# A backbone of two layers on one core: the way from the first attention into its FFN put in a set order, the latents' norm first, two inner tiles multiplied feature by feature, unread modulation rows left out

## The chip, the cores and the metric

The kernel runs on one core of one Trainium2 chip. The metric is the device time of one execution in microseconds, as the median of several runs.

A core has five engines that run beside each other: TensorE (PE in the profile) multiplies and writes into PSUM, VectorE (DVE) and ScalarE (ACT) work element by element, GpSimd (POOL) here adds and issues some transfers, SyncE (SP) issues loads. An engine runs its instructions in the order in which they stand in its queue; one that waits holds up all that stand behind it.

## The reference, cut to what matters

512 latent tokens `x` and 256 context tokens `ctx`, of 1024 features, go through two layers. Each layer has attention and a SwiGLU feed-forward network (FFN, 2816 inner features), each behind a norm that is scaled and shifted by modulation vectors. Latents and context have modulation of their own.

```python
for layer in range(2):
    mod_x = split(silu(c)     @ ada_w[layer] + ada_b[layer], 6)     # for latents
    mod_c = split(silu(c_ctx) @ ada_w[layer] + ada_b[layer], 6)     # for the context
    h_x = modulate(rmsnorm(x, norm_g[layer, 0]), mod_x[0], mod_x[1])
    h_c = modulate(rmsnorm(ctx, norm_g[layer, 0]), mod_c[0], mod_c[1])
    o_x, o_c = mixer(h_x, h_c, ...)                                 # o_c only in layer 0
    x = x + mod_x[2] * o_x
    h_x = modulate(rmsnorm(x, norm_g[layer, 1]), mod_x[3], mod_x[4])
    x = x + mod_x[5] * ((silu(h_x @ w1) * (h_x @ w3)) @ w2)
    if layer == 0:
        ctx = ctx + mod_c[2] * o_c
        h_c = modulate(rmsnorm(ctx, norm_g[layer, 1]), mod_c[3], mod_c[4])
        ctx = ctx + mod_c[5] * ((silu(h_c @ w1) * (h_c @ w3)) @ w2)
return rmsnorm(x, final_g)
```

In layer 1 the context gets no output, so of its six modulation rows only the first two (`mod_c[0]`, `mod_c[1]`) are read.

## The kernel before

**Layout.** Activations lie with features on the 128 partitions, in KT = 8 tiles `k` of 128 features, and tokens along the free dimension: NX = 512 latents and NC = 256 context tokens. `xr` and `cr` are the residual streams, `hx` and `hc` (tiles `hb0` to `hb7`) the normed inputs. Everything is held as a high and a low part, and each product is made of three, `mm3`: high weight by high input (L209), high by low (L210), low by high (L211).

**Weights.** A `Stream` S loads raw weight tiles of 128 x 1024 in a fixed order (SP), and makes the two parts: high by ACT (L160 or L198), low by DVE as raw minus high (L161 or L199, the tile `wl`). A second way, `split_by_dma`, takes DVE out of it: ACT writes minus the rounded raw values into the low tile (L203), a transfer issued on POOL adds raw to them in place (L204, `wl<-raw`), and ACT writes the high part (L205).

**The end of the first attention.** The output projection has eight chunks `m` of 128 output features (`wo_chunk`). The second half of each is multiplied here: for `t` = 0 to 3 the latents' products of m = 2t and 2t + 1 (the context's of the chunks m > 1 are held back). Each ends with a residual addition on DVE (L1324), after which ACT squares the residual and DVE or POOL add the squares up (`sq_sum`: L334, L338, L340). Two sums are kept apart, so the statistics product (`rstd_of`, L308) has two matmuls for the latents and two for the context. Then `rstd_from` and for each feature tile `h_make`: a product with scale and rstd on DVE (L352), the high part on ACT (L353), the low part on DVE (L354).

**Into the FFN.** Inner tiles `j` of 128 features: `plain_tile` multiplies w1 and w3 of the tile with latents and context, takes silu (L1518 or L1520) and multiplies (L1522), and splits the result g. For j = 0 PE gets sixteen keep-busy matmuls (L219) that are issued behind the last context product. j = 0 to 3 are done in this way, then comes `seven` for each later pair of inner tiles: seven products of 384 tokens instead of eight (L1533 to L1535), from sums of token halves (`token_sums`, L1468 to L1486, with the splits of T) that DVE and ACT make while tiles 2 and 3 are multiplied.

**Modulation rows.** The modulation vectors of the later steps are made on the side: for a load of 128 x 1024 of the transposed `ada_w` DVE multiplies with the latents' conditioning row and sums (L271), then with the context's (L272). I call each of the two a half row. Three groups of them lie near the change: four late rows of layer 0 under the output projection (`late_rows`), four at the start of the FFN (`rows(4, ...)`), the other rows of layer 1 spread over the FFN up to 911 us.

**What sets the order.** The program is written in Python under a scheduler that places the instructions of each engine by its own estimates, within the dependencies; `issue_after` adds one. PSUM has eight banks. Each new tile in a bank waits for the last reader of the tile before it. SBUF memory is handed on in the same way.

## Time and profile before

| | us |
|---|---|
| median of 3 runs (1574.49 to 1578.61) | 1577.53 |
| the profiled execution | 1577.44 |
| its span | 1575.6 |
| PE, DVE, ACT, POOL busy | 1540.2, 1228.7, 728.8, 257.1 |
| PE idle between 415.2 and 490.1 (end of the output projection, norms, inner tiles 0 and 1) | 4.15 |
| PE idle between 490.1 and 523.4 (inner tiles 2 and 3) | 0.0 |

All times in a profile are from one execution, counted from the start of the span. An instruction's time has a tail in which the next one has begun: wide matmuls (512 columns) follow each other every 0.23 us and show 0.39. Line numbers are those of the kernel before where nothing else is said. The changed file is longer, and a line that is the same in both has another number there: L1324 there is L1344, or L1417 where it is written out anew; L1468 is L1673, L1522 is L1723, L271 and L272 are both L274, and L1533 is L1734.

### The profile page before, as it was taken

The numbers are of one execution on the slowest core, as the hardware profiler recorded it, in microseconds if no ns is written. First come the engines' busy times: TensorE is split into PE (matmuls) and PEld (weight loads), VectorE is DVE, ScalarE is ACT, GpSimd is POOL, SyncE is SP. The second block draws the span as 40 slices with busy tenths as digits, with TensorE's granted clock in tenths as the row PEclk, the third lists the DMA queues.
The fourth block names the chain that finished last, engine by engine and source line by source line (L and its number), as shares of the span: only waits on it lengthen the run. The fifth ranks groups of instructions, "written<-read, shape, count | busy, mean of one in ns | idle before, by whom it ended". The sixth has DMA issues, their size and how long they took to land.

```text
span 1575.6 us, 25696 instructions
## 1 busy us (share of the span) xinstructions
PE 1540.2 (98%) x10021; PEld 1369.0 (87%) x10021; DVE 1228.7 (78%) x2097; ACT 728.8 (46%) x1241; POOL 257.1 (16%) x329
## 2 busy tenths in 40 slices
PE   9999999999999999999999999999999999999997
PEld 5898988877778999999999998877778899989897
DVE  4768788967698789869799777677666887869686
ACT  4556554445354523433425244366655543425344
POOL 1033213552010000010100002255430000000000
PEclk9999999999999999999999999999999999999999
DMA  9422254633235465485766752311113442422321
GB/s 357 113 61 85 83 162 138 203 111 101 65 120 165 117 178 157 139 209 160 203 178 162 214 149 92 91 55 41 42 41 87 128 147 81 134 68 94 121 81 54
DMA packets 68625, 196.41 MB, mean 125 GB/s; under 512 B 6692, under 2 KB 19140, under 8 KB 68504
## 3 DMA queue, kind: packets, MB, share of 16 engines
q1 hardware_dynamic: 58040, 159.95, 31.9%
q0 software_dynamic: 9488, 33.51, 9.8%
q8 instruction: 79, 1.29, 0.3%
q10 hardware_dynamic: 976, 1.31, 0.3%
q14 instruction: 42, 0.34, 0.1%
HBM read 161.04 MB, written 4.86 MB: 105 GB/s over the span
## 4 chain that ended last, share of the span: by engine, by line
PE 51%; DVE 6%; issue 5%; DMA 4%; ACT 1%; POOL 0%; SPq 0%; DVEq 0%; POOLq 0%; ACTq 0%
PE f L1535 4%; PE f L1534 4%; PE f L1533 4%; PE f L2208 4%; PE f L2209 4%; PE f L2210 4%; PE f L1574 2%; PE f L1575 2%; PE f L1576 2%; PE lin L1870 2%; PE s L1759 2%; PE f L2262 2%; PE f L2263 2%; PE f L2261 2%; PE t L410 2%
## 5 line engine op out<-in xcount | busy, mean ns | idle before, releaser
L198 ACT ACTIVATE wh<-raw 128x1024 fp32r<-128x1024 f32 (+1 forms) x96 | 92.1, 977 | 235.1 <-DVE raw L539 88.7
L199 DVE TENSOR_TENSOR wl<-raw,wh 128x1024 fp32r<-128x1024 f32 (+1 forms) x96 | 106.9, 1120 | 39.7 <-ACT wh L198 39.1
L209 PE MATMUL lin<-hb,wh 128*128 128x512 f32 (+1 forms) x352 | 121.7, 347 | 5.5 <-DVE k L379 2.0
L210 PE MATMUL lin<-hb,wh 128*128 128x512 f32 (+1 forms) x352 | 120.2, 342 | 0.4 <-DVE hb L1303 0.4
L211 PE MATMUL lin<-hb,wl 128*128 128x512 f32 (+1 forms) x352 | 119.0, 338 | 0.0
L271 DVE SCALAR_TENSOR_TENSOR junk<-raw,tables 128x1024 bf16<-128x1024 f32 x80 | 99.4, 1243 | 19.1 <-DMA raw<-in_ada_wT_dram 18.7
L204 POOL DMA_DIRECT2D wl<-raw x39 | 34.1, 873 | 443.9 <-ACT wl L203 404.1
L1574 PE MATMUL f<-g,wh 128*128 128x512 f32 (+1 forms) x304 | 102.4, 338 | 0.4 <-DVE s L1563 0.4
L1575 PE MATMUL f<-g,wh 128*128 128x512 f32 (+1 forms) x304 | 102.8, 339 | 0.0
L2209 PE MATMUL f<-hb,wh 128*128 128x256 f32 x360 | 101.6, 283 | 0.0
L2208 PE MATMUL f<-hb,wh 128*128 128x256 f32 x360 | 101.4, 283 | 0.0
L2210 PE MATMUL f<-hb,wl 128*128 128x256 f32 x360 | 101.2, 283 | 0.0
L1576 PE MATMUL f<-g,wl 128*128 128x256 f32 (+1 forms) x304 | 101.1, 337 | 0.0
L1535 PE MATMUL f<-hb,wl 128*128 128x384 f32 x288 | 96.3, 334 | 0.0
L1533 PE MATMUL f<-hb,wh 128*128 128x384 f32 x288 | 96.2, 334 | 0.0
L1534 PE MATMUL f<-hb,wh 128*128 128x384 f32 x288 | 96.2, 334 | 0.0
L209 PEld LDWEIGHTS lin<-hb,wh 128*128 128x128 f32 x352 | 66.6, 189 | 16.9 <-issue 2.7
L1535 PE MATMUL f<-T,wl 128*128 128x384 f32 x216 | 72.3, 336 | 2.2 <-DVE wl L199 2.2
L210 PEld LDWEIGHTS lin<-hb,wh 128*128 128x128 f32 x352 | 66.7, 189 | 8.2 <-DVE hb L1303 0.6
L211 PEld LDWEIGHTS lin<-hb,wl 128*128 128x128 f32 x352 | 66.6, 189 | 7.5
L1534 PE MATMUL f<-T,wh 128*128 128x384 f32 x216 | 72.2, 334 | 0.0
L1533 PE MATMUL f<-T,wh 128*128 128x384 f32 x216 | 72.2, 334 | 0.0
(540 smaller groups left out, 4843.3 us busy)
## 6 DMA issues: line engine op xcount, KB each, us to landing
raw<-in_w_dram SPq DMA_DIRECT2D x132, 512.0 KB, 3.7
raw<-in_ada_wT_dram SPq DMA_DIRECT2D x80, 512.0 KB, 3.8
wl<-raw POOLq DMA_DIRECT2D x41, 512.0 KB, 6.5
raw<-in_w_ab_dram SPq DMA_DIRECT2D x24, 512.0 KB, 4.3
raw<-in_w_c_dram SPq DMA_DIRECT2D x12, 512.0 KB, 4.3
raw<-in_ada_w_dram SPq DMA_DIRECT2D x8, 512.0 KB, 9.2
nb<-in_na_bias_dram POOLq DMA_DIRECT2D x16, 256.0 KB, 3.2
raw<-in_wo_ab_dram SPq DMA_DIRECT2D x8, 512.0 KB, 3.9
```

The costliest lines, as they stand in the source:

```text
L209: nc.tensor.matmul(ps, wh(k), xh(k), start=k == 0, stop=False)
L210: nc.tensor.matmul(ps, wh(k), xl(k), start=False, stop=False)
L211: end = nc.tensor.matmul(ps, wl(k), xh(k), start=False, stop=k == n - 1)
L1533: nc.tensor.matmul(ps, wh(k), b[:, 0, :], start=k == 0, stop=False)
L1534: nc.tensor.matmul(ps, wh(k), b[:, 1, :], start=False, stop=False)
L1535: nc.tensor.matmul(ps, wl(k), b[:, 0, :], start=False, stop=k == 3)
L1574: nc.tensor.matmul(ps, hi, g[:, 0, cols[v]], start=first, stop=False)
L1575: nc.tensor.matmul(ps, hi, g[:, 1, cols[v]], start=False, stop=False)
L1576: nc.tensor.matmul(ps, lo, g[:, 0, cols[v]], start=False, stop=last)
L2208: nc.tensor.matmul(ps, wh(k), b[:, 0, :], start=k == 0, stop=False)
L2209: nc.tensor.matmul(ps, wh(k), b[:, 1, :], start=False, stop=False)
L2210: nc.tensor.matmul(ps, wl(k), b[:, 0, :], start=False, stop=k == 3)
```

## The change

1. The order between the last chunks of the output projection and the end of tiles 0 and 1 is written out by hand for PE, DVE and ACT (`manual_schedule`).
2. The latents' residuals come first; their squares are summed on ACT and DVE alone, into one sum, so that one matmul makes the statistics (L1485). The context's chunks 2 to 7 are multiplied while the norm's chain runs.
3. w1 and w3 of inner tiles 0 and 1 are placed in memory of the attention's work tiles (`spare`, tile `w0`), and split with an ACT copy and an accumulating transfer on POOL (L1456, L1457, L1459). Their products with the latents are made for one feature tile at a time, as each h is there (`first_products`, L1541), into four banks `s`. The context's products follow (`lin`). The sixteen keep-busy matmuls go.
4. The attention's PSUM pools stay open until tiles 0 and 1 are done; the FFN's eight banks are opened behind that, on the same memory.
5. In layer 1 the half rows of the context for s = 2 to 5 are left out (`sides`). Three late rows instead of four are under the output projection, one more is left to the FFN (`rows(5, ...)`, now behind `token_sums` in the program).
6. The next conversions of weights (pair p = 1 and one of p = 2) are issued behind the norm's end (`behind_norm`), and the two rope loads of the next norm behind a residual addition.

PE behind the last context product of the output projection, before (`lin`: a bank of the attention, `f`: a bank of the FFN, `hb0`, `hb1`: normed inputs, `wh` and `wl`: high and low weights, f_4836 and f_4838 w1 and w3 of tile 0, f_4977 w1 of tile 1):

```order
L211 MATMUL lin_4689<-hb7_121,wl_4488 128x256
L219 MATMUL f_4836<-ones_96,ident_95 128x128 x16
L308 MATMUL t_4703<-ns_a_4704,ones_96 128x256
L308 MATMUL t_4703<-ns_a_4705,ones_96 128x256
L209 MATMUL f_4836<-hb0_114,wh_4860 128x512
L209 MATMUL f_4838<-hb0_114,wh_4864 128x512
L209 MATMUL f_4977<-hb0_114,wh_4981 128x512
L210 MATMUL f_4836<-hb0_114,wh_4860 128x512
```

Now the first product L1541 stands right behind the context's last one (`s_4697<-hb0_114,w0_4546`); twelve products for features 0 and 1 of tile 0 come, and then tile 1 begins. Their end (s_4697 is tile 0, s_4698 tile 1; w0_4546 holds both parts of w1 of tile 0, 4547 and 4548 the parts of w3; 4549 and 4550 those of w1 of tile 1, 4551 and 4552 those of w3):

```order
L1541 MATMUL s_4697<-hb1_115,w0_4548 128x512
L1541 MATMUL s_4697<-hb1_115,w0_4546 128x512
L1541 MATMUL s_4697<-hb1_115,w0_4547 128x512
L1541 MATMUL s_4698<-hb0_114,w0_4549 128x512
L1541 MATMUL s_4698<-hb0_114,w0_4551 128x512
L1541 MATMUL s_4698<-hb0_114,w0_4550 128x512
L1541 MATMUL s_4698<-hb0_114,w0_4552 128x512
```

The keep-busy products and the context's statistics no longer stand ahead of the first h. The 16th of the new products is the first that reads w0_4552, the low part of w3 of tile 1.

ACT at the norm's end, now (`ns_h`: input times scale and rstd; rows L1456 write a low part, L1459 a high one; no such rows stood there before):

```order
L1456 ACTIVATE w_4550<-raw 128x1024
L1459 CAST w_4549<-raw 128x1024
L1400 ACTIVATE ns_h<-res 128x256
L1525 ACTIVATE hb_114<-ns_h,mod_110 128x512
L1525 ACTIVATE hb_115<-ns_h,mod_110 128x512
L1456 ACTIVATE w_4552<-raw 128x1024
L1525 ACTIVATE hb_116<-ns_h,mod_110 128x512
L1459 CAST w_4551<-raw 128x1024
```

The last low part stands behind the latents' features 0 and 1, and what POOL adds to it comes behind that.

DVE between the context's last h and the token sums, before (half rows: L271, L272 with the output `junk`; `q<-f`: the product of silu and w3's output; `g`: its low part; L1468: the first token sum):

```order
L271 SCALAR_TENSOR_TENSOR junk_4817,mod0_110<-raw_4820,tables_72 128x1024
L272 SCALAR_TENSOR_TENSOR junk_4817,mod0_110<-raw_4820,csr1_4791 128x1024
L271 SCALAR_TENSOR_TENSOR junk_4817,mod0_110<-raw_4824,tables_72 128x1024
L272 SCALAR_TENSOR_TENSOR junk_4817,mod0_110<-raw_4824,csr1_4791 128x1024
L1522 TENSOR_TENSOR q_5101<-f_4979,q_5101 128x512
L274 TENSOR_TENSOR mod0_110<-mod0_110,adab_104 128x16
L1522 TENSOR_TENSOR q_5101<-f_4980,q_5101 128x256
L199 TENSOR_TENSOR wl_5181<-raw_4996,wh_5180 128x1024
L199 TENSOR_TENSOR g_4835<-q_5101,g_4835 128x768
L1468 TENSOR_TENSOR q_5111<-hb0_114 128x768
```

Now, from tile 1's product on:

```order
L274 SCALAR_TENSOR_TENSOR junk_4985,mod0_110<-raw_4981,tables_72 128x1024
L1723 TENSOR_TENSOR q_4994<-s_4698,q_4994 128x512
L536 TENSOR_TENSOR res_4975<-raw_5141 128x512
L1723 TENSOR_TENSOR q_4994<-lin_4915,q_4994 128x256
L274 SCALAR_TENSOR_TENSOR junk_4985,mod0_110<-raw_4981,csr1_4983 128x1024
L537 TENSOR_TENSOR raw_5141<-raw_5141,raw_5139 128x512
L199 TENSOR_TENSOR wl_5401<-res_4975,wh_5400 128x512
L199 TENSOR_TENSOR g_4986<-q_4994,g_4986 128x768
L274 SCALAR_TENSOR_TENSOR junk_4985,mod0_110<-raw_5097,tables_72 128x1024
```

All eight half rows stood ahead of tile 1's product; now three of ten do, and seven come behind it, the last five of them between the token sums.

The core of the diff:

```diff
+    def sides(l, s):
+        return 1 if l and s > 1 else 2
...
     def ada_rows(l, s, k, cs, raw, junk):
-        col = mod[l][:, s, :, k : k + 1]
-        nc.vector.scalar_tensor_tensor(junk, raw, 1.0, cs[0], op0=ALU.mult, op1=ALU.mult, accum_out=col[:, 0])
-        nc.vector.scalar_tensor_tensor(junk, raw, 1.0, cs[1], op0=ALU.mult, op1=ALU.mult, accum_out=col[:, 1])
+        col, n = mod[l][:, s, :, k : k + 1], sides(l, s)
+        for i in range(n):
+            nc.vector.scalar_tensor_tensor(junk, raw, 1.0, cs[i], op0=ALU.mult, op1=ALU.mult, accum_out=col[:, i])
...
+    def behind_norm(fn):
+        def f(raw):
+            with tc.issue_after(norm_end[0].ins):
+                return fn(raw)
+        return f
...
-                        late_rows += row_pieces(1)
+                        late_rows.append(row_pieces((2, 1, 0, 0)[m - 4]))
...
-        r = rstd_of(tp(), sq_sum(xr, nmap), D, nmap)
-        for k in range(KT):
-            h_make(k, hx[k], xr[k], r, 0, 1, 0, nmap)
-        weights0()
-        for m, w in held:
-            wo_chunk(m, w, "c", 4)
...
+        def conversion(hi, lo):
...
+            def low():
+                nc.scalar.activation(lo, raw, AF.Copy, scale=-1.0)
+                nc.gpsimd.dma_start(f32(lo), raw, accum_op=ALU.add)
+            return low, lambda: nc.scalar.copy(hi, raw)
+
+        w10, w30, w11, w31 = (conversion(*z) for z in spare)
+        by_hand = ExitStack()
+        by_hand.enter_context(tc.manual_schedule(engines={ENG.PE, ENG.DVE, ENG.Activation}))
...
+        nc.tensor.matmul(psx, ones, ax[0], start=True, stop=True)
...
+        first_ps = [[[s[:, NX * i : NX * i + NX], None] for i in range(2)] for s in (sp2(), sp2())]
+
+        def first_products(*jk):
+            for j, k in jk:
+                for kind in ("hh", "lh", "hl"):
+                    for i in range(2):
+                        w = wslice(first_w[2 * j + i][kind == "lh"])
+                        nc.tensor.matmul(
+                            first_ps[j][i][0], w(k), hx[k][:, int(kind == "hl"), :],
+                            start=k == 0 and kind == "hh", stop=k == KT - 1 and kind == "hl",
+                        )
+
+        h_t(0, 0)
+        h_t(1, 0)
+        w31[0]()
+        h_lo(0, 0)
+        to_residual(5, 1, pc[5])
+        h_t(2, 0)
+        w31[1]()
+        square(5, 1)
+        h_lo(1, 0)
+        first_products((0, 0))
...
+        first_products((0, 1), (1, 0))
...
+        first_products((0, 6), (1, 5), (0, 7), (1, 6), (1, 7))
...
         def plain_tile(j, g):
...
-            if j == 0:
-                keep_busy(ps[0][0], 16, before[0])
...
+            if j < 2:
+                ps = first_ps[j]
             else:
...
-        rows(4, h_made[-1][1])
+        g = g_tile()
+        for j in range(2):
+            plain_tile(j, g)
+        banks.close()
+        for i in range(8):
+            fpp.pools.append(st.enter_context(tc.tile_pool(name=f"f_ps{i}", bufs=1, space=PSUM, reuse_waits="tile")))
+        token_sums()
+        rows(5, h_made[-1][1])
```

More of the change, by code (lines that the diff above doesn't have):

```diff
@@ L221, in keep_busy @@
                 nc.tensor.matmul(ps[:, 0:P], ident, ones, start=True, stop=True)
-    before = [None]
     def wo_slices(t, i):
@@ new lines, in tile_trunk @@
+        first_products((0, 2), (1, 1))
+        add_square(6, 1)
+        add_halves(1)
+        h_t(5, 0)
+        h_lo(4, 0)
+        first_products((0, 3), (1, 2))
+        add_square(7, 1)
+        psc = tp()[:, 0:NC]
+        first_products((0, 4), (1, 3))
+        nc.tensor.matmul(psc, ones, ac[0], start=True, stop=True)
+        h_t(6, 0)
+        h_lo(5, 0)
+        first_products((0, 5), (1, 4))
+        chain = stats(psc, NC, place[2][:, 0:NC], rstds[1], place[2][:, NC:NX])
+        next(chain)
@@ L1399, in tile_trunk @@
+        by_hand.close()
     with ExitStack() as st:
```

234 lines of the change are left out of this document (182 added, 52 removed).

## The prediction

> **What bounds the kernel now.** The page first: which engine is busy, and which one the chain that ended last runs over.
>
> ```profile
> span 1575.6 us, 25696 instructions
> PE 1540.2 (98%) x10021; PEld 1369.0 (87%) x10021; DVE 1228.7 (78%) x2097; ACT 728.8 (46%) x1241; POOL 257.1 (16%) x329
> PE 51%; DVE 6%; issue 5%; DMA 4%; ACT 1%; POOL 0%; SPq 0%; DVEq 0%; POOLq 0%; ACTq 0%
> ```
>
> TensorE (PE) is busy 98% of the span, so a change pays only through its idle time and through products that are not work. Next the table by stage around the change; after the stage's bounds stand its length, then busy time and instructions of PE, PEld, DVE, ACT and POOL, the granted clock, DMA share and GB/s.
>
> ```profile
> 415.20:490.10 74.90, 70.75 (x405) 60.86 (x404) 62.42 (x103) 32.61 (x54) 7.83 (x7) 1.00 0.40 118
> 490.10:523.40 33.30, 33.30 (x194) 29.47 (x193) 31.28 (x56) 14.87 (x23) 1.72 (x2) 1.00 0.45 132
> 475.00:500.00 25.00, 25.00 (x154) 22.49 (x153) 18.00 (x30) 10.52 (x14) 1.80 (x2) 1.00 0.73 212
> 500.00:525.00 25.00, 25.00 (x148) 22.38 (x147) 24.58 (x45) 12.69 (x21) 1.72 (x2) 1.00 0.35 85
> 725.00:750.00 25.00, 23.28 (x134) 22.94 (x133) 23.34 (x41) 10.33 (x12) 0.87 (x1) 1.00 0.48 135
> ```
>
> The passage, from the second half of the output projection to the end of tiles 0 and 1, runs from 415.2 to 490.1; PE idles 74.90 - 70.75 = 4.15 us in it. Tiles 2 and 3 (490.1 to 523.4) have no gap, but DVE is busy 31.28 of 33.30 us under them. So two engines are close to the bound here, one behind the other. The timeline of PE shows the places (start, duration, then in brackets the idle time before):
>
> ```profile
> 442.99 1.88 PE L308 MATMUL t<-ns_a,ones 128*128 128x512 f32 x4
> 449.01 3.73 PE L219 MATMUL f<-ones,ident 128*128 128x128 f32 x32
> 453.48 1.10 PE L308 MATMUL t<-ns_a,ones 128*128 128x256 f32 x4 [0.73 <-DVE ns_a L340]
> 457.36 0.50 PE L210 MATMUL f<-hb,wh 128*128 128x512 f32 x1 [1.60 <-DVE hb L354]
> 490.12 0.40 PE L209 MATMUL f<-hb,wh 128*128 128x512 f32 x1
> 523.49 0.34 PE L1533 MATMUL f<-hb,wh 128*128 128x384 f32 x1
> ```
>
> The sixteen keep-busy products take 3.73 us, and the largest gap is 1.60. Tile 2 starts at 490.12, the first "seven" product (that of token pair 2 and 3) at 523.49. These two times are the marks of my sum.
>
> **What can be gained in the passage.** Gaps 4.15, keep-busy products 3.73, and half of the two statistics products ((1.88 + 1.10) / 2 = 1.49): 9.4 us, if PE then never waits. All other products stay.
>
> **New waits, one by one.** (1) In the new order the latents' statistics product comes behind the context products of m = 2 and 3 (about 440.2 on this axis), then the context products of m = 4 to 7, then the first product L1541, which needs the first h. The rows on its way:
>
> ```profile
> 444.91 0.69 ACT L315 ACTIVATE ns_t<-t,epst 128x512 f32<-128x512 f32 x1 [0.92 <-PE t L308]
> 446.36 0.61 ACT L317 ACTIVATE ns_y<-ns_t 128x512 f32<-128x512 f32 x1
> 447.81 0.62 ACT L318 ACTIVATE ns_t<-ns_y 128x512 f32<-128x512 f32 x1
> 456.57 0.74 DVE L354 SCALAR_TENSOR_TENSOR hb<-ns_h,mod,hb 128x512 fp32r<-128x512 f32 x1
> 454.03 0.72 ACT L353 ACTIVATE hb<-ns_h,mod 128x512 fp32r<-128x512 f32 x1 [2.25 <-DVE ns_h L352]
> 478.11 1.06 ACT L203 ACTIVATE wl<-raw 128x1024 fp32r<-128x1024 f32 x1
> ```
>
> The product takes 0.94 with its tail, ACT 0.69 + 0.61 + 0.62, DVE three rows of 0.74, ACT 0.72 for h: 5.8, and 1.4 for DVE rows of the context that stand in between and for hand-overs: h is there at 447.4. PE has 0.66 of statistics and 4 x 1.44 of context products (a tile's pass of 24 wide and 24 narrow products is 33.3 / 4 = 8.3, so a narrow one is 0.12, a wide one 0.23): 446.6. A wait of 0.8. Waits for residual rows and the next h rows stay near those of before: 1.4 together.
>
> (2) The weights of tiles 0 and 1 get their low halves not from DVE (four subtractions of 1.2 us, freed) but from an ACT copy and an accumulating DMA issued on POOL. The last of the four (w3 of tile 1) has its copy (1.06) behind h of features 0 and 1 on ACT, so from 448.0 to 449.0, and is issued at about 449.3. The 16th L1541 product needs it, 15 x 0.23 and two short waits behind the first: 451.3. What does such a DMA take? Count, KB, median us to landing, for the whole page, then for the stages 460 to 500 and 500 to 540:
>
> ```profile
> wl<-raw POOLq DMA_DIRECT2D x41, 512.0 KB, 6.5
> wl<-raw POOLq DMA_DIRECT2D x2, 512.0 KB, 7.0
> wl<-raw POOLq DMA_DIRECT2D x5, 512.0 KB, 4.5
> ```
>
> At 449 one weight load and the copy of the conditioning row run beside it in the new order, less than from 460 on, more than from 500 on: I take 5.5, with bounds 4.5 and 7.0. The product waits 449.3 + 5.5 - 451.3 = 3.5 us (2.5 to 5.0). [...] Sum for tiles 0 and 1: -9.4 + 0.8 + 1.4 + 3.5 = -3.7, so they end at 486.4 instead of 490.1.
>
> (3) Tile 2's first product takes a bank of the freed attention pools, the one that tile 1's gate product (L1723) reads last. Before, eight separate banks were there and nothing waited. The elementwise work costs:
>
> ```profile
> 489.99 0.68 DVE L1522 TENSOR_TENSOR q<-f,q 128x512 f32<-128x512 f32 x1
> 480.00 0.96 DVE L199 TENSOR_TENSOR g<-q,g 128x768 fp32r<-128x768 f32 x1 [0.50 <-ACT g L198]
> 479.07 0.83 ACT L198 ACTIVATE g<-q 128x768 fp32r<-128x768 f32 x1
> 481.06 0.60 ACT L1520 ACTIVATE q<-f 128x512 f32<-128x512 f32 x1 [1.16 <-DVE g L199]
> 474.13 1.22 DVE L272 SCALAR_TENSOR_TENSOR junk<-raw,csr 128x1024 bf16<-128x1024 f32 x1
> ```
>
> After tile 1's last product: tile 0's high half 0.83 on ACT, its low half 0.96 on DVE, then tile 1's silu 0.60, a half row of the modulation that stands in between (started about 0.7 before the silu is through, so another 0.6), the multiplication 0.68, with 0.3 of hand-overs: 4.0 us. Tile 2 starts at 490.4, against 490.12. The gain of the passage is used up at that place; bounds 2.7 (no half row in the way) and 5.3 (two).
>
> (4) Tiles 2 and 3 take their 33.3 us and are done at 523.7. What they cover before is DVE's token sums (L1468 and on) and the splits of T:
>
> ```profile
> 487.57 1.22 DVE L271 SCALAR_TENSOR_TENSOR junk<-raw,tables 128x1024 bf16<-128x1024 f32 x1 [4.19 <-DMA raw<-in_ada_wT_dram]
> 493.43 1.83 DVE L1468 TENSOR_TENSOR q<-hb 128x768 f32<-128x768 f32 x2
> 497.50 0.69 DVE L534 TENSOR_TENSOR res<-raw 128x512 f32<-128x512 f32 x1 [1.78 <-DMA raw<-in_w_dram]
> 519.88 0.85 ACT L1520 ACTIVATE q<-f 128x512 f32<-128x512 f32 x2
> ```
>
> Before, all eight half rows of this place had run by 490, in a stretch where DVE had time to wait 4.19 us for a load. Tile 2's silu, which frees the bank of the first seven product, came at 519.88, behind the T splits; with 0.65 for its first half it was through at 520.5, only 3.0 us ahead of PE's need at 523.49. In the changed order the rows come through two fresh buffers whose loads wait for memory that tile 1 reads until about 478, and seven half rows stand behind tile 1's multiplication, among the token sums: 7 x (1.22 + 0.04 read-out and gap) = 8.8 us. From tile 1's multiplication (490.4): the rest of the tile and one half-size conversion 3.0, the half rows 8.8, sums and splits as before (519.88 + 0.65 - 493.43 - 1.78 of waiting = 25.3, less 2.0 of conversions now ahead of it, plus 1.2 for one now in it), and 1.3 for L540, which waits for an accumulating DMA that has become late with the rest: 528.0. PE waits 4.3 us there, and starts at 528.0 instead of 523.49: +4.5. Bounds: L540's wait 0 to 3 and the landing in (2), together -2.3 to +3.2, and (3)'s, up to +1.3: +4.5.
>
> (5) Later. In layer 1 the context's half of rows s = 2 to 5 is left out: 32 of the half rows of this group (min, median, max in ns, first and last start).
>
> ```profile
> L272 DVE SCALAR_TENSOR_TENSOR junk<-raw,csr x52: 1207/1218/1229, 474.1 to 910.9; 128x1024 bf16<-128x1024 f32 x52
> 575.00:600.00 25.00, 24.53 (x142) 24.21 (x141) 23.45 (x40) 9.47 (x10) 1.74 (x2) 1.00 0.70 200
> 600.00:625.00 25.00, 24.57 (x141) 22.33 (x140) 23.21 (x41) 8.50 (x9) 0.87 (x1) 1.00 0.51 141
> 734.29 0.44 PE L1535 MATMUL f<-T,wl 128*128 128x384 f32 x1 [1.72 <-DVE wl L199]
> ```
>
> That takes 39 us from DVE up to 911. PE could use it in three places: 0.47, 0.43 and 1.72 us of idle time. So 0 to -2.6; I take half, -1.3, since DVE also starts this stretch 4 us later. The rope tables' loads and the five conversions put behind the norm lie under 33 us of products: nothing.
>
> **Sum.** +4.5 - 1.3 = +3.2. The profiled execution took 1577.4 (span 1575.6 and 1.8 around it), 0.1 below the median of 1577.53, so I forecast 1580.5. Within its own bounds (-2.3 and -1.3 below, +4.5 and +1.3 above): 1577 to 1586. A change of 0.3% (4.7 us, 1572.8 to 1582.3) is about what can be told from none.
>
> **Rivals.** *The gain stays (faster).* The half rows load earlier or fall into DVE's wait before tile 0's silu (about 475 to 481, when it has no other work), and the token sums are then covered. The half row drops out of (3), the 8.8 out of (4), so PE no longer waits at the first seven product: 486.4 - 1.0 (a landing of 4.5) + 2.7 + 33.3 = 521.4, that is -2.1; the later -2.6 makes it 1572.7, and if DVE's 4.9 us freed in (2) close the small waits of (1) too, 1571.3. For it: the 4.19 us that DVE waits for a load now. Against it: their order on DVE, which is fixed.
>
> *The accumulating DMA or the row loads come late (slower).* The stage 460 to 500 has a median of 7.0 where the row loads run at the same time, and 475 to 500 has the highest DMA share, 0.73. With 7.0 at all of them the product in (2) waits 1.5 more and L540 1.5 more, and a late row load holds DVE's queue for 1 to 2: +3.2 + 4.5, 1585. It decides from a landing of about 6.3 on.
>
> *The clock falls (slower).* The keep-busy products go, and two waits of 4 us come. The clock as the profile grants it (third column from the right), at the start, at the gaps of the passage and at the end:
>
> ```profile
> 12.00:16.00 4.00, 3.37 (x6) 1.74 (x7) 2.11 (x5) 2.19 (x4) 0.00 (x0) 0.62 1.04 384
> 453.00:457.00 4.00, 2.06 (x7) 1.16 (x7) 4.00 (x7) 2.97 (x6) 0.00 (x0) 1.00 0.87 294
> 1568.00:1572.00 4.00, 0.00 (x0) 0.00 (x0) 3.35 (x6) 0.23 (x1) 0.00 (x0) 0.68 0.29 97
> ```
>
> With 1.94 us idle of four the clock stays at 1.00, with four idle it falls (0.68), and at 12 to 16 it is 0.62 though PE is busy. If each of the two waits is followed by such a stretch, four microseconds at 0.62, each costs 1.5 more: 1580.5 + 3.0 = 1583.5. [...]
>
> **Chances.** Within 0.3% (the sum as it stands): 0.42. The gain stays: 0.22, faster. Late DMAs 0.24 and the clock 0.12: slower, 0.36. The range of 1571 to 1588 leaves out about 0.1 at each end: it reaches below the first rival and holds the second with the clock's price on top.
>
> **What would show it.** In the profile after: no L219; the first L1541 product near 447 and a PE wait of about 3.5 us for a DMA of w<-raw fifteen products later; tile 2's first product near 490 behind a DVE L1723; half rows (L274) among L1673 and L1681 from 491 to 509; a PE wait of about 4 us at the first L1734 product, near 528. Step (2) is wrong if that DMA lands in under 4 us or over 7, step (4) if PE has no wait of over 2 us at L1734, step (5) if the time between that product and 911 shrinks by over 2.6 us or grows. The clock rival needs a granted clock under 1.00 right after one of these waits.

## The result, and the profile after

| | us |
|---|---|
| predicted | 1580.5 (1571 to 1588) |
| after, median of 6 runs (1584.92 to 1603.48) | 1593.36 |
| before, median of 6 runs beside them (1574.49 to 1579.97) | 1577.38 |
| after / before | 1.0106, interval 1.0072 to 1.0139 |
| the profiled execution of after, and its span | 1594.26, 1592.5 |

The change makes the kernel 16 us slower. The forecast had it within 0.3% and missed by 12.9 us, outside its range.

The top of the page of after, in answer to the first fence of the prediction:

```profile
span 1592.5 us, 25552 instructions
PE 1543.6 (97%) x9985; PEld 1371.8 (86%) x9985; DVE 1190.2 (75%) x2035; ACT 733.4 (46%) x1245; POOL 255.9 (16%) x329
PE 64%; DMA 13%; DVE 10%; issue 8%; ACT 4%; SPq 0%; POOL 0%; DVEq 0%; ACTq 0%; POOLq 0%
```

PE has 36 matmuls less and yet 3.4 us more busy time, and 13.5 us more of idle time (1592.5 - 1543.6 = 48.9 against 35.4). DVE lost 38.5 us of work, near the 39 foreseen, and the end came no earlier. In the last chain, DMA went from 4% to 13%.

The timeline of PE in after, the rows that answer to the marks (start, duration, the idle time before it in brackets; L1541 are the products made feature by feature, L209 at 493.35 is tile 2's first, L1734 the first "seven" product):

```profile
448.55 4.03 PE L1541 MATMUL s<-hb,w 128*128 128x512 f32 x14 [0.60 <-ACT hb L1525]
452.94 0.50 PE L1541 MATMUL s<-hb,w 128*128 128x512 f32 x1 [0.36 <-DMA w<-raw]
456.52 11.65 PE L1541 MATMUL s<-hb,w 128*128 128x512 f32 x39 [3.08 <-DMA w<-raw]
493.35 0.79 PE L209 MATMUL f<-hb,wh 128*128 128x512 f32 x1 [3.67 <-DVE q L1723]
533.48 0.60 PE L1734 MATMUL f<-hb,wh 128*128 128x384 f32 x1 [3.66 <-ACT q L1721]
927.22 0.69 PE L1736 MATMUL f<-hb,wl 128*128 128x384 f32 x1 [4.82 <-DMA wl<-raw]
```

Three of the four waits are those of the forecast, at their places and in their sizes (3.4, 3.67, 3.66; forecast 3.5, 4.0, 4.3). The fourth, at 927, was not in it. But the marks are late: tile 2 starts 3.2 us later than before (493.35 against 490.12), the first seven 10.0 (533.48 against 523.49), the span ends 16.9 later. So 10.0 us are lost ahead of the first seven and 6.9 behind it. The clock tells more. The columns are those of the prediction's stage table, in windows of 2 us behind the waits:

```profile
456.00:458.00 2.00, 1.48 (x4) 1.19 (x5) 2.00 (x4) 0.72 (x1) 0.00 (x0) 0.50 0.81 291
460.00:462.00 2.00, 2.00 (x6) 1.52 (x6) 0.00 (x0) 0.00 (x0) 0.00 (x0) 0.52 0.20 76
462.00:464.00 2.00, 2.00 (x11) 1.62 (x10) 0.00 (x0) 0.00 (x0) 0.00 (x0) 1.00 0.00 0
494.00:496.00 2.00, 2.00 (x6) 1.59 (x5) 0.00 (x0) 0.00 (x0) 0.00 (x0) 0.50 0.72 272
534.00:536.00 2.00, 2.00 (x8) 2.00 (x7) 2.00 (x4) 1.30 (x2) 0.00 (x0) 0.50 0.00 0
928.00:930.00 2.00, 2.00 (x8) 2.00 (x8) 2.00 (x5) 1.27 (x2) 0.00 (x0) 0.50 0.00 0
```

Behind each of the four waits the granted clock is 0.50 (third column from the right), up to 461.9 behind the first: six products in 2 us instead of eleven. PE counts as busy there. PE's busy time at 0.50, multiplied by the half that the clock lacks, is 2.70, 3.06, 1.71 and 2.87 us, 10.34 in all.

Now the wait at 927. POOL's timeline in after (L204 is the accumulating transfer, L1652 the rope loads):

```profile
892.78 0.87 POOL L204 DMA_DIRECT2D wl<-raw  x1 [7.57 <-ACT wl L203]
919.04 1.13 POOL L1652 DMA_DIRECT2D tables<-in_rope_dram  x2 [25.39 <-DVE junk L274]
920.14 0.96 POOL L204 DMA_DIRECT2D wl<-raw  x1
```

The ACT copy ahead of that last transfer, and the DVE instruction that waits for it, from the timelines of ACT and DVE:

```profile
912.34 1.05 ACT L203 ACTIVATE wl<-raw 128x1024 fp32r<-128x1024 f32 x1
927.20 0.69 DVE L540 TENSOR_TENSOR raw<-res,raw 128x512 f32<-128x512 f32 x1 [5.73 <-DMA wl<-raw]
```

And POOL at the same place before, where the rope loads are L1446 and L1447:

```profile
903.46 0.87 POOL L204 DMA_DIRECT2D wl<-raw  x1 [20.04 <-ACT wl L203]
910.19 0.57 POOL L1446 DMA_DIRECT2D tables<-in_rope_dram  x1 [5.86 <-DVE junk L271]
918.03 0.90 POOL L204 DMA_DIRECT2D wl<-raw  x1 [6.72 <-ACT wl L203]
```

The transfer that goes out at 903.46 before, ahead of the rope loads, stands behind them after. The loads overwrite the conditioning row that the last half row reads, so they wait 25.39 us for it, and the L204 behind them is issued at 920.14 although its ACT copy was through at 913.4. Counted over the program, 37 L204 are ahead of the rope loads before, 36 after. In these rows POOL issues in the order of its queue, the loads at 919.04 and the L204 behind them at 920.14: loads that nobody needed yet held up a transfer for which PE waited 4.82 us and DVE 5.73.

### The profile page after: what moved, and what is told of

It is laid out like the page before. It is cut to its first block, busy times and chain, and to the rows that moved or that the text cites. A ratio compares the mean times of both kernels' runs of the same rounds, so it can differ in the third digit from the quotient of the medians.

```text
span 1592.5 us, 25552 instructions
## 1 busy us (share of the span) xinstructions
PE 1543.6 (97%) x9985; PEld 1371.8 (86%) x9985; DVE 1190.2 (75%) x2035; ACT 733.4 (46%) x1245; POOL 255.9 (16%) x329
## 4 chain that ended last, share of the span: by engine, by line
PE 64%; DMA 13%; DVE 10%; issue 8%; ACT 4%; SPq 0%; POOL 0%; DVEq 0%; ACTq 0%; POOLq 0%
DMA wl<-raw 6%; PE f L2415 4%; PE f L2414 4%; PE f L2413 4%; PE lin L209 3%; PE f L1736 3%; PE lin L211 3%; PE f L1735 3%; PE f L1734 3%; PE lin L210 3%; PE t L412 3%; PE f L1775 3%; PE f L1777 3%; PE f L1776 3%; DVE junk L274 2%
## 5 line engine op out<-in xcount | busy, mean ns | idle before, releaser
L199 DVE TENSOR_TENSOR wl<-raw,wh 128x1024 fp32r<-128x1024 f32 (+1 forms) x96 | 106.9, 1122 | 46.4 <-ACT wh L198 45.8
L209 PE MATMUL lin<-hb,wh 128*128 128x512 f32 (+1 forms) x344 | 118.8, 346 | 4.8 <-DVE k L381 2.5
L210 PE MATMUL lin<-hb,wh 128*128 128x512 f32 (+1 forms) x344 | 118.1, 343 | 0.5 <-DVE hb L1323 0.5
L274 DVE SCALAR_TENSOR_TENSOR junk<-raw,tables 128x1024 bf16<-128x1024 f32 x77 | 95.7, 1243 | 14.1 <-DMA raw<-in_ada_wT_dram 13.9
L204 POOL DMA_DIRECT2D wl<-raw x39 | 34.0, 873 | 439.0 <-ACT wl L203 421.6
L1734 PE MATMUL f<-hb,wh 128*128 128x384 f32 x288 | 98.0, 340 | 3.7 <-ACT q L1721 3.7
L1735 PE MATMUL f<-hb,wh 128*128 128x384 f32 x288 | 98.0, 340 | 0.0
L209 PEld LDWEIGHTS lin<-hb,wh 128*128 128x128 f32 x344 | 65.1, 189 | 15.4 <-DVE k L381 3.3
L1734 PE MATMUL f<-T,wh 128*128 128x384 f32 x216 | 72.1, 334 | 0.0
L210 PEld LDWEIGHTS lin<-hb,wh 128*128 128x128 f32 x344 | 65.1, 189 | 8.1 <-DVE hb L1323 0.7
```

The lines of the kernel that those rows point to most:

```text
L209: nc.tensor.matmul(ps, wh(k), xh(k), start=k == 0, stop=False)
L210: nc.tensor.matmul(ps, wh(k), xl(k), start=False, stop=False)
L1734: nc.tensor.matmul(ps, wh(k), b[:, 0, :], start=k == 0, stop=False)
L1735: nc.tensor.matmul(ps, wh(k), b[:, 1, :], start=False, stop=False)
```

## The experiments

All runs in one table; the interval belongs to the ratio to before, which was run beside each on the same chip.

| | what is changed | median us (runs) | ratio | interval |
|---|---|---|---|---|
| e1_clock | after, keep-busy products in two of the waits | 1592.04 (6) | 1.0092 | 1.0075 to 1.0109 |
| e2_rope | after, rope loads one L204 later | 1585.16 (6) | 1.0050 | 1.0035 to 1.0065 |
| e3_feat | after, tile 1's products begin later | 1585.32 (6) | 1.0052 | 1.0034 to 1.0069 |
| e4_rows | after, five rows behind the token sums | 1586.68 (6) | 1.0058 | 1.0043 to 1.0073 |
| e6_bothsides | after, unread half rows back | 1584.61 (6) | 1.0045 | 1.0031 to 1.0059 |
| e7_all | e2 + e3 + e4 + order of banks | 1587.48 (6) | 1.0062 | 1.0046 to 1.0078 |
| e8_rows_clock | e4 + e1 | 1588.99 (6) | 1.0066 | 1.0048 to 1.0083 |
| b1_nobusy | before, no keep-busy products | 1578.89 (12) | 1.0009 | 0.9998 to 1.0020 |
| b2_sides | before, unread half rows left out | 1586.60 (6) | 1.0053 | 1.0038 to 1.0067 |
| b3_sides_rope | b2, rope loads one L204 later | 1579.99 (12) | 1.0014 | 1.0004 to 1.0023 |
| b4_early | before, its four rows moved ahead | 1579.58 (12) | 1.0012 | 1.0000 to 1.0025 |
| c3 | e2 + e3 + order of banks | 1585.24 (5) | 1.0049 | 1.0035 to 1.0062 |
| c3_norows | c3 without the five rows | 1574.11 (12) | 0.9978 | 0.9968 to 0.9987 |
| c4 | c3, two of five rows moved ahead | 1579.44 (10) | 1.0024 | 1.0012 to 1.0036 |
| c5 | c3, four of five moved ahead | 1574.30 (12) | 0.9995 | 0.9986 to 1.0004 |
| c6 | c3, all five moved ahead | 1578.68 (12) | 1.0008 | 0.9996 to 1.0019 |
| x1_norows | e2 without the five rows | 1579.08 (12) | 1.0025 | 1.0014 to 1.0036 |
| x2_norows_busy | x1 + e1 | 1577.31 (12) | 1.0005 | 0.9993 to 1.0017 |

The kernel before has medians of 1575.42 to 1578.39 us on the chips of these runs, so rows are best compared by their ratios. The interval of after itself (1.0072 to 1.0139) is about 5 us wide to each side, and a gain over after is known no better than that; the intervals of e1, e4, e7 and e8 overlap with it. Where a size matters, the marks of the profiled executions are given beside the medians.

### The rope loads

**e2_rope** puts the two rope loads behind one more accumulating transfer; `accs` is the list of these in the program's order.

```diff
-                with tc.issue_after(end.ins):
+                with tc.issue_after(end.ins), tc.issue_after(accs[-4].ins):
                     nc.gpsimd.dma_start(t, src)
```

> The changed kernel with one thing moved: on POOL's queue the two rope loads of the next norm stand behind one more accumulating transfer, 37 ahead of them as in the kernel before instead of 36. Theory A: the rope loads wait for the last half row of the modulation (918.7 us), and the transfer that stands behind them is issued at 920.1 instead of 913.5, which makes PE wait 4.8 us at 922.4 and halves its clock for 5.5 us behind that. Then both go: 4.8 + 2.9 = 7.7 us less, to about 1585.5. Rival B: the transfer would be late anyway (its raw tile or the DMA engines), and only 0 to 2 us go. Rival C: the clock falls whatever the wait, then 4.8 go and not 7.7: 1588.5.

1585.16 us, 8.2 less than after. POOL's timeline at the place:

```profile
911.25 0.87 POOL L204 DMA_DIRECT2D wl<-raw  x1 [20.04 <-ACT wl L203]
915.12 1.13 POOL L1652 DMA_DIRECT2D tables<-in_rope_dram  x2 [3.00 <-DVE junk L274]
```

The window of e2 in which PE waits and then runs at half clock in after:

```profile
920.00:925.00 5.00, 5.00 (x31) 5.00 (x30) 4.92 (x8) 2.05 (x3) 0.00 (x0) 1.00 0.33 105
```

The transfer goes out 8.9 us earlier (911.25 against 920.14) and PE has no gap. From the first seven to the end the profiled execution takes 1051.8 us, against 1059.0 in after and 1052.1 before. The order on POOL explains about half of the loss, all that lies behind the first seven.

**e6_bothsides** and **b2_sides** ask what moved the loads. The first computes the unread half rows again, the second leaves them out of the kernel before and changes nothing else.

```diff
     def sides(l, s):
-        return 1 if l and s > 1 else 2
+        return 2
```

> The changed kernel with one part undone: the unread half rows of layer 1 are computed again. In its order on POOL the rope loads stand behind 37 accumulating transfers, as in the kernel before. Theory A: leaving the rows out cost 7.7 us net through the rope loads' place, so it takes 1584.5 to 1586.5, and what is left over the kernel before (7 to 8 us) is the passage's. Rival B: the rows left out gain their 1 to 2.6 us in the FFN and the place of the loads costs little: 1594 to 1596.

```diff
+    def sides(l, s):
+
+        return 1 if l and s > 1 else 2
...
-        col = mod[l][:, s, :, k : k + 1]
-        nc.vector.scalar_tensor_tensor(junk, raw, 1.0, cs[0], op0=ALU.mult, op1=ALU.mult, accum_out=col[:, 0])
-        nc.vector.scalar_tensor_tensor(junk, raw, 1.0, cs[1], op0=ALU.mult, op1=ALU.mult, accum_out=col[:, 1])
+        col, n = mod[l][:, s, :, k : k + 1], sides(l, s)
+        for i in range(n):
+            nc.vector.scalar_tensor_tensor(junk, raw, 1.0, cs[i], op0=ALU.mult, op1=ALU.mult, accum_out=col[:, i])
```

> The kernel before with one part of the change alone: the context's half rows for s = 2 to 5 of layer 1 are left out. In its order on POOL the two rope loads stand behind 36 accumulating transfers instead of 37, as in the changed kernel. Theory A: leaving out 39 us of DVE's work saves 1 to 2.6 us in the FFN, but the transfer behind the rope loads is held up until the last half row, PE waits 3 to 5 us near 915 and loses 2.9 more by its clock: 1582 to 1585. Rival B: the rows end earlier here, so the rope loads hold nothing up: 1575 to 1576.5.

With 39 us of DVE work back, the changed kernel is 8.7 us faster (1584.61). Without that work, the kernel before is slower by 0.53% (0.38 to 0.67%). From the waits of PE in b2 (what waited, for what; us in total, times, longest):

```profile
PE f L1539 <- DMA wl<-raw: 4.2, 2, 3.6
```

The window of b2 with the end of that wait:

```profile
915.00:920.00 5.00, 4.04 (x13) 4.04 (x14) 4.02 (x7) 2.00 (x2) 0.00 (x0) 0.51 0.01 2
```

The same wait as in after, with the same fall of the clock, in a kernel that has nothing else of the change; its rope loads also stand behind 36 transfers. So it is the removal of work that moved the loads. The likely reason is that the scheduler places them by its estimate of when their buffer comes free, which is earlier with the half rows gone; no run shows these estimates.

**b3_sides_rope** is b2 with the loads put back behind 37, as in e2.

> The kernel before with the unread half rows left out, as in the run that gave 1586.6, and the two rope loads put back behind 37 accumulating transfers on POOL. Theory A: the whole loss of that run came from the one transfer that stood behind the rope loads (a wait of 3.6 us near 912 and 7 us at half clock behind it). Then the time is 1574 to 1577, not slower than the kernel before (1577.9). Rival B: fewer rows change the order elsewhere, and 3 us or more of the loss stay: 1581 or above.

1579.99: most of the loss is gone, but no gain is left, rather 0.14% (0.04 to 0.23%) of loss. 39 us less of DVE work between 530 and 911 are worth next to nothing: PE's waits between the first seven and 965 us come to 2.8 us, against 2.6 before, and from the first seven to the end the profiled execution takes 1051.2 us, 0.9 less than before.

### The clock and the waits

**e1_clock** fills two waits with products that nobody reads: 13 ahead of the first product that needs the late low part, 14 behind tile 1's last.

```diff
-                        w = wslice(first_w[2 * j + i][kind == "lh"])
+                        w = wslice(first_w[2 * j + i][kind == "lh"]); keep_busy(idle, 13 if (j, k, kind, i) == (1, 0, "lh", 1) else 0)
...
-        by_hand.close()
+        keep_busy(tp(), 14); by_hand.close()
```

> The changed kernel with keep-busy products put back into two of its waits: 13 of them ahead of the 16th first product (the wait of 3.1 us for the low part of w3 of tile 1), 14 behind the last context product of tile 1 (the wait of 3.7 us for tile 1's gate product). They take 0.233 us each and write a bank that nothing reads. Theory A, the clock: each wait of over 3 us halves the granted clock for 5 to 6 us behind it and costs 2.8 us more than the wait itself. Then the waits stay, the clock stays at 1.00 behind these two, the first products take 0.23 us each instead of 0.30, and the time falls by 5.6 us, to about 1588. Rival B, the waits alone cost the time: no change within 1 us, 1593. Rival C, the products delay what follows: 0 to 1 us slower.

1592.04, 1.3 less than after and not told apart from it, where theory A had 1588; the range of its runs is 1590.01 to 1593.71, that of after 18.6 us wide. The window of e1 behind the first wait:

```profile
455.00:460.00 5.00, 5.00 (x31) 4.40 (x30) 3.42 (x7) 1.45 (x2) 0.00 (x0) 1.00 0.87 307
```

And from e1's waits of PE:

```profile
PE f L1734 <- ACT q L1721: 6.7, 1, 6.7
```

In the profile the clock stays at 1.00 through both waits. Tile 2 starts at 490.81, 2.5 us earlier, and the first seven comes 2.3 earlier (531.14). The fall behind tile 2's start is gone too, 3.1 us, but that only makes PE's wait at the first seven longer, by 3.0. So in these two executions the fall ahead of tile 1's end counts, since DVE's work starts from there; the one behind it does not, since DVE sets the first seven.

**e3_feat** takes the wait itself away. Tile 1's products begin when tile 0 has had four features instead of two, so the late low part is needed later.

```diff
-        first_products((0, 1), (1, 0))
+        first_products((0, 1))
...
-        first_products((0, 3), (1, 2))
+        first_products((0, 3), (1, 0), (1, 1), (1, 2))
```

> The changed kernel with the first products in another order: tile 0 goes on with features 2 and 3, and tile 1 begins behind these (its features 0, 1 and 2 one after the other) instead of after feature 1 of tile 0. So the low part of w3 of tile 1 is needed about 3 us later. Theory A: the wait of 3.1 us is replaced by waits under 1 us for h of features 2 and 3, and the clock does not fall: 3.1 - 1.0 + 2.8 = 4.9 us less, to about 1588.5. Rival B: the next wait (tile 1's gate product before tile 2) takes it up, because DVE and not PE sets that time: under 1 us less. Rival C: the waits for h add up to the same idle time without a fall of the clock: 2.8 less, 1590.5.

1585.32, a gain of 8.0 where 5 was expected. There is no wait for `w<-raw` any more, and the clock is 1.00 from 450 to 460. Tile 2 starts at 488.68, 4.7 us earlier, and DVE's chain with it, so that the first seven is 4.3 earlier:

```profile
529.14 0.69 PE L1734 MATMUL f<-hb,wh 128*128 128x384 f32 x1 [5.26 <-ACT q L1721]
```

Of the rest, 1.7 is at the rope loads, where PE's wait is 3.1 instead of 4.8, and 1.4 is the stretch at half clock behind it, which is half as long.

**e4_rows** moves the five rows at the FFN's start behind the last split of the token sums.

```diff
-        rows(5, h_made[-1][1])
+        rows(5, sums_end[0])
```

> The changed kernel with the five rows at the start of the FFN (ten half rows of 1.26 us on DVE) issued behind the last split of the token sums instead of behind the norm. Theory A: the seven half rows among the token sums hold up the first seven product (PE waits 3.7 us at 533.5) and one more stands ahead of tile 1's gate product. Then the wait at the first seven product goes, the clock stays at 1.00 behind it: 3.7 + 2.0 = 5.7 us less, and 0.6 at tile 2: to about 1587. Rival B: the ten half rows come later all the same, and hold up a later product by as much: under 1.5 us less. Rival C: the silu that frees the bank stands behind the splits on ACT whatever DVE does: 2 us less.

1586.68 as expected (1587). The first seven comes at 528.30 and without a wait, while the waits of the passage and the one at 927 are still there. **e8_rows_clock** adds the products of e1 to it, so that PE now also wins in the passage.

> The rows moved behind the token sums (as in the run before, 1586.7) and the keep-busy products in the two waits (as in the other run, where 2.2 us won by 493 were taken up at the first seven product). Now nothing waits at that product, so the clock's price can show. Theory A: 2.8 us for the stretch at half clock from 455 to 461 and 2.9 for that from 492 to 498: 1581. Rival B: the fall of the clock costs nothing that the next wait does not take up: 1586 to 1587.

1588.99, where 1581 was expected. The first seven is early (524.65). But the clock falls for 3.41 us at 452.57 in spite of the keep-busy products, behind a wait of 1.43 ahead of them, and new waits show from 542 on, for low parts of token sums that the next products read (`hb`), which DVE makes (L199) with the moved rows in between:

```profile
PE f L1735 <- DVE hb L199: 2.7, 3, 1.0
```

Among these waits the clock falls once more, for 6.83 us from 544.73, which takes 2.8 us of PE's time.

**e7_all** puts e2, e3 and e4 together and gives tile 2 a bank that comes free earlier.

```diff
-        token_sums()
+        fpp.pools = [fpp.pools[i] for i in (6, 7, 0, 1, 2, 4, 3, 5)]; token_sums()
```

> The changed kernel with four repairs together: the rope loads behind one more accumulating transfer; tile 1's first products behind features 2 and 3 of tile 0; the five rows at the FFN's start behind the token sums; and the FFN's eight banks taken in another order, so that tile 2's first product gets a bank of the statistics and not the one that tile 1's gate product reads last. Theory A: no wait of over 1 us and no fall of the clock is left from 440 to 930. The waits of 3.1, 3.7, 3.7 and 4.8 us and 10.5 us of half clock go: tile 2 starts near 484, the first seven product near 517.5, and the time is 1570 to 1572, 6 us under the kernel before. Rival B: DVE sets the time at the first seven product whatever PE gains; then it starts near 522 and the time is 1575 to 1577.

1587.48. Neither theory had it: PE has no wait of over 0.6 us from 449 to 518, and the first seven is at 520.4, 3.1 us earlier than before the change. But all ten moved half rows are run between 521.5 and 544.7, and among them stand the next token sums (L1690 to L1692) and their splits:

```profile
PE f L1735 <- DVE hb L199: 6.1, 2, 3.4
PE f L1734 <- ACT hb L198: 2.4, 2, 1.8
```

With these waits the clock is at 0.50 for 13.65 us from 539.75, which takes another 3.4 us of PE's time. Moved rows are not removed rows: behind the first seven they are in the way of the next.

### How much of it is DVE at the first seven

**c3** is e7 with the rows left where after has them, and **c3_norows** leaves them out.

```diff
-        rows(5, h_made[-1][1])
```

> The changed kernel with three of the four repairs (rope loads, features, banks) and the half rows at their place among the token sums. Theory A (DVE sets the time of the first seven product): tile 2 starts at 484.5 without a wait, and PE then waits 6 to 9 us at the first seven product, which starts at 526 to 527 as DVE gets through, with a fall of the clock behind it: 1579 to 1582. Rival B (PE sets it): the wait there stays at 3.7 us and the gain of 7 us from the earlier tile 2 comes out: 1573 to 1575.

> The same kernel without the five rows at the FFN's start: their loads and ten half rows (12.6 us of DVE) are left out, and the gates that they make are set to 0.5, so the output is another one. It shows what DVE holds up. Theory A: without them nothing waits from 440 to 560: the first seven product starts near 518, and the time is 1566 to 1570. Rival B: DVE's token sums and splits alone are as late, and PE waits 3 us or more there all the same: 1573 or above.

1585.24 and 1574.11, both above their theory A (1579 to 1582, 1566 to 1570). The first seven on c3's timeline of PE:

```profile
529.27 0.69 PE L1734 MATMUL f<-hb,wh 128*128 128x384 f32 x1 [12.49 <-ACT q L1721]
```

And the same wait in c3_norows, where that product starts at 519.65:

```profile
PE f L1734 <- ACT q L1721: 2.0, 1, 2.0
```

In c3 no wait of over 0.5 us holds PE between tile 0's start and 516, and then it waits for all of what it won: 12.5 us. Without the five rows the wait is 2.0. **c4** and **c5** move two and four of them into unit 6 of the attention's eight (counted from 0; the last that makes such rows), ahead of the output projection, **c6** all five; the core of c5:

```diff
-                n1, n2 = (4, 4) if u > 3 else (0, 0)
+                n1, n2 = (4 + 2 * (u == 6), 4 + 2 * (u == 6)) if u > 3 else (0, 0)
...
-        rows(5, h_made[-1][1])
+        rows(1, h_made[-1][1])
```

> The three repairs (rope loads, features, banks) with two of the five rows computed earlier, as two more rows in the last unit of the first attention (near 350, where DVE is busy 13.5 to 17.6 us of 25). Three rows stay at the FFN's start: four half rows ahead of tile 1's product, two later, one or two of them among the token sums. Theory A (DVE's backlog sets the first seven product): 5 to 6 us less than with five rows there (1585.2), 1579 to 1580, and the attention loses 0 to 1. Rival B: the rows cost the attention what they save here: 1584 or above.

> The same with four rows earlier, in the last unit of the first attention, and one row left at the FFN's start, its half rows ahead of tile 1's product. Theory A: nothing of the rows stands among the token sums, so it comes within 1 to 2 us of the kernel that leaves them out (1574.1): 1575 to 1577, under the kernel before by 1 to 2 us. Rival B: 10 us of DVE in the attention cost PE 3 us or more there: 1579 or above.

> The three repairs, with all five rows of the FFN's start computed in the last unit of the first attention, so that no half row is left between the norm and the token sums. Theory A: the wait of 2.4 us at the first seven product and the stretch at half clock behind it (about 1.5 us) go, and the attention loses under 1 us: 2 to 3 us less than with four rows there (1574.3 beside 1575.4 for the kernel before), 0.998 to 0.999 of the kernel before. Rival B: the wait stays, since it is the token sums' own and not the rows': 0.9995 as with four.

The wait at the first seven goes 12.5, 7.1, 2.4, 2.0 with five, three, one and no row there: 2.5 us a row for the first four, two half rows of 1.22 and their gaps. The last one is worth 0.4, since from there the token sums themselves set the time. c5, 0.9995 (0.9986 to 1.0004), is the best full version and not told apart from before; c6 is not told apart from c5 either. In its profiled execution the way from the first new product to the first seven is 0.9 us shorter than in c5 (71.0 against 71.9), but the first new product comes at 450.95 instead of 447.53; why it is late was not followed up. **b4_early** moves the rows of the kernel before in the same way:

> The kernel before with its four rows at the FFN's start computed in the last unit of the first attention, nothing else changed. Theory A: there these rows lay in DVE's free time (it waited 4.2 us for one of their loads), so nothing is gained, within 1 us of the kernel before; what the repaired kernels win by moving the rows is owed to the change's order. Rival B: the rows cost DVE time that PE waits for in the kernel before too: 2 to 4 us faster.

1579.58: nothing is gained, PE had no wait there that could go.

### The price of a fall of the clock

**x1_norows** is e2 without the five rows, so that DVE is not late at the first seven; **x2_norows_busy** adds the keep-busy products of e1 to it.

> The changed kernel with the rope loads put behind 37 accumulating transfers and without the five rows at the FFN's start (their loads and half rows are left out, the gates that they make are 0.5, so the output is another one). DVE no longer holds up the first seven product, so what PE loses ahead of it comes through. The waits for the low part of w3 (about 3 us) and for tile 1's gate product (2.5 to 3.7 us, the half row in it is gone) stay, each with its fall of the clock. Theory A: 1574.1 (the same with all of the waits repaired) + 3 + 3 + 2 x 2.8 = 1582 to 1586 less what was waited there anyway: 1581. Rival B: DVE's token sums still decide, and it takes 1575 to 1577.

> The same kernel as x1_norows (rows left out, other output) with the keep-busy products in the two waits. The waits stay as long, only the clock is held up. Theory A: each fall of the clock behind a wait costs 2.8 us, so this is 5 to 6 us faster than x1_norows on the same chip. Rival B: the fall costs nothing of its own, since what follows waits for DVE: within 1 us of x1_norows.

A window of x1 behind the waits for the accumulating transfer:

```profile
455.00:460.00 5.00, 3.00 (x7) 2.15 (x7) 4.82 (x9) 2.36 (x4) 0.00 (x0) 0.51 0.95 240
```

The same window of x2:

```profile
455.00:460.00 5.00, 5.00 (x30) 4.29 (x29) 2.92 (x5) 1.45 (x2) 0.00 (x0) 1.00 0.77 288
```

From the first L1541 product to the first seven, x1 takes 80.2 us and x2 75.8: 4.4 us, in two profiled executions. But x1's profiled one was its slowest run (1584.67), and the medians, 1579.08 and 1577.31, differ by 1.8, more than rival B's 1 and less than theory A's 5 to 6. The falls of the passage cost between 1.8 and 4.4 us, and by the scatter not the same in every run. Which part of after's 18.6 us of scatter is theirs, these runs do not say.

**b1_nobusy** asks the same of the kernel before: its sixteen keep-busy products are left out.

```diff
-            if j == 0:
-                keep_busy(ps[0][0], 16, before[0])
```

> The kernel before without its sixteen keep-busy products, nothing else. PE is then idle for 4.5 us from 449.0 to 453.5, and after two short statements for 0.2 and 1.6 us more. Theory A (the clock): it falls to 0.50 for some 5 us behind that and costs 2.5 to 4 us: 1580 to 1581.5. Rival B: the products only filled a wait, and leaving them out changes nothing: 1577 to 1578. Rival C: they held up the statistics, 1 us less.

From the waits of PE in b1, the place where the keep-busy products were:

```profile
PE t L308 <- DVE ns_a L340: 4.3, 1, 4.3
```

And the first of the two windows behind it:

```profile
450.00:455.00 5.00, 1.82 (x5) 1.51 (x5) 5.00 (x10) 1.69 (x3) 0.21 (x1) 0.80 0.84 261
```

PE idles 4.3 us, the clock falls to 0.80 and 0.86 in two windows of 5 us (3.41 us at 0.50, from 452.97 on), and the kernel takes 1578.89, 0.09% more (-0.02 to 0.20%). The fall is nearly free here: PE's next waits for h shrink by about as much (the one at L210 from 1.60 to 0.56), and from the latents' statistics product to the first seven both kernels take 80.5 us.

## Why the prediction was wrong, step by step

**(1) The norm ahead of the first product.** Wait 0.8 forecast, 0.60 measured. The product came at 448.55 instead of 447.4; that mark lies between 446.85 and 449.52 in the runs whose code is the same up to there, so this is no miss.

**(2) The accumulating transfer.** The answer on transfers for 446 to 460:

```profile
w<-raw POOLq DMA_DIRECT2D x2, 512.0 KB, 6.5
```

I took 5.5, within 4.5 to 7.0. The 6.5 is the median of two; the one that the 16th product waits for is issued at 450.40 and lands 6.1 later. The wait was 3.44 (3.08 and 0.36), forecast 3.5. The mechanism is right; that the size fits to 0.1 is luck, since the transfer took 0.6 longer and PE also came to the product 0.6 later than forecast, counted from the first new product.

**(3) The bank for tile 2.** Wait 4.0 forecast, 3.67 measured. The start, 490.4 in the forecast, is 490.81 in e1, where the clock does not fall, and 493.35 in after. The step is right; what it lacked is the clock. Its lower bound of 2.7 was too low: only 0.6 of the half row was in the sum of 4.0, so without it 3.4 is left, and in e4 and x1, where no half row stands there, the wait is 3.28.

**(4) DVE's half rows among the token sums.** There are seven behind tile 1's multiplication, as forecast. The stretch from tile 2's start, at the end of that multiplication, to the first seven was to take 37.6 us and took 40.1. The term that was mis-sized is a load, which I had taken out as a wait of before that would go. DVE in after:

```profile
492.61 0.68 DVE L1723 TENSOR_TENSOR q<-s,q 128x512 f32<-128x512 f32 x1
496.90 0.69 DVE L536 TENSOR_TENSOR res<-raw 128x512 f32<-128x512 f32 x1 [3.60 <-DMA raw<-in_w_dram]
523.06 0.69 DVE L540 TENSOR_TENSOR raw<-res,raw 128x512 f32<-128x512 f32 x1 [0.71 <-issue]
```

The wait was 1.78 before, counted as zero in the sum, and is 3.60 now; in the runs with rows in place it is 2.6 to 4.7. L540, for which I had put 1.3, waits 0.71. With the start 3.0 later (493.35 instead of 490.4) the first seven is 5.5 later than forecast, +10.0 instead of +4.5. The mechanism was right: c3, c4 and c5 show that DVE sets this time, row by row.

**(5) Later.** "The rope tables' loads ... lie under 33 us of products: nothing." This is the step that failed. The 33 us are tiles 2 and 3, and the rope loads do not lie there: they go out at 910.19 before and at 919.04 in after. I had asked what covers the loads, and not what stands behind them on POOL while they wait, and had not counted that the order there could change with the work left out. It cost some 8 us: 8.2 by e2, 8.7 by e6 and 6.6 by b2 against b3. And the gain of 0 to 2.6 us for DVE's 39 us was put at 1.3; by b3 it is none in the median and 0.9 at most in the profile. Behind the first seven the forecast had 1.3 us less than before, and the profiled execution has 6.9 more: 8.2 of the miss are this step.

**The rival of the clock** had 0.12 and 3.0 us. Its mechanism is what happened, four times instead of twice. Its price was read off the row at 12 to 16 us, a mean of 0.62 over 4 us, so 1.5 each. That row averages over an edge: the clock before is 0.50 from 12.93 on for 3.41 us. Behind the first wait of after it was 0.50 for 6.83 us, 5.4 of them with PE at work, so 2.7. My condition, a gap near four, asked for too much: in after the clock fell behind 3.08 with 0.36 just before it. On the time of the kernel the four falls do not add up to their 10.3 us: e1 takes the first two away, 5.8 us, and gains 2.5 in the profiled executions, 1.3 in the medians; the fourth is part of the 8 us of (5).

**The other rivals.** The transfer that held PE landed after 6.1, short of the 6.3 from which that rival was to decide, and what it said of the row loads did not come. The gain did not stay: even with all waits of the passage over 0.6 us gone (c3) PE waits for DVE.

**The sum.** Of the 16 us, 8 are the order on POOL. The other 8 are the passage and the first seven, where the forecast had +4.5; the rest is DVE's wait for the load and its later start behind the first fall. In the profiled executions the two parts are 6.9 and 10.0, and the miss is 8.2 and 5.5. (By its own terms the forecast was 0.1 low: 1577.4 + 3.2 is 1580.6.) The gains of e2, e3 and e4 (8.2, 8.0, 6.7) add up to more than there is, and c3, with two of them, is no faster than either: PE and DVE take turns at the same places, so they cannot be added. How the second 8 us divide between the clock and DVE, to the microsecond, stays open.

## What to carry to other kernels

Work that is left out moves what a scheduler places around it; compare each queue's order before and after, and for each transfer that moves ask what stands behind it while it waits. A gain on PE is worth what the engine behind it can follow: with DVE busy 31.3 of 33.3 us under the next stage (before, 490.1 to 523.4), the first four rows put there came back as 2.5 us of wait each (12.5 in c3, 2.4 in c5). Here the clock fell behind waits of 2.4 us (c5), 3.66 and 4.82 (after) for one or two steps of 3.41 us; price a new wait of PE of this length with a chance of such a fall, and ask whether the next stage is waiting for PE at all.

## What the runs showed of the hardware

- In these profiles the clock fell in steps of 3.41 us. The stretches at 0.50, but for the one at the end, last 3.41 or 6.83 us in before and after; in e7 one lasts 13.65, and in c3 one lasts 10.3 by its windows (520 to 525 at 0.69, 525 to 530 at 0.50, 530 to 535 at 0.78). In after the starts lie 11, 12 and 115 times 3.413 us apart. The four of after:

```profile
455.09:461.92 6.83, 5.40 (x13) 4.24 (x14) 3.75 (x8) 1.55 (x3) 0.00 (x0) 0.50 0.72 237
492.64:499.47 6.83, 6.12 (x14) 4.79 (x15) 3.23 (x8) 1.36 (x2) 0.00 (x0) 0.50 0.56 221
533.60:537.01 3.41, 3.41 (x11) 3.41 (x12) 3.41 (x6) 1.90 (x3) 0.00 (x0) 0.50 0.00 0
926.13:932.96 6.83, 5.74 (x18) 5.74 (x19) 5.72 (x10) 2.00 (x2) 0.00 (x0) 0.50 0.08 15
```

They cost 1.71 (one step) to 3.06 us (two) of PE's time in after. The length of a wait alone did not tell whether a fall came: behind one of 2.0 us the clock fell in c6 (0.70 from 520 to 525, 0.96 from 525 to 530) and behind one of 1.98 it stayed at 1.00 in c3_norows (514 to 524). It fell behind 2.4 in c5 (0.72 from 520 to 525), and in x1 behind two waits of 1.24 and 2.00 with a single product between them (0.51 from 455 to 460). What decides it, no run shows.
- An accumulating transfer of 512 KB took 6.5 us at the median from 446 to 460 in after, where the DMA engines' share was 0.96, against 4.5 from 500 to 540 before (share 0.35 from 500 to 525).
- In after the rope loads' issue, which waited for DVE (L274), held POOL's queue for 25.39 us. POOL counts as idle for that time (0.00 us busy from 893.65 to 919.04), and only the bracket tells.
